# One-bank accumulators and a fixed order of copies, casts and sums in the first chunk of an up projection

## The chip, the cores and the metric

The kernel runs on one core of a Trainium2 chip. The metric is the time of one execution in microseconds (us): the median of three runs before the change is 1266.63 us (1265.53 to 1266.91). One execution was also taken by the hardware profiler: it lasted 1267.56 us, of which its span, from the first to the last instruction, is 1265.8 us.

## The reference

One decoder layer in float32 over 1024 tokens and 16 prepended meta tokens, width 1024. What matters here is its last third, the ConvFFN:

```python
up = causal_dwconv(h @ ffn_w_up, ffn_dw, ffn_dw_b)      # 1024 -> 2 * 2816, then 3 taps
u, g = jnp.split(up, 2, axis=-1)
f = (jax.nn.gelu(g, approximate=False) * u) @ ffn_w_down
return layer_norm(DEEPNORM_ALPHA * h + f, ln2_g, ln2_b)
```

`h` is the output of the first layer norm, which follows the product with `w_out`. All the rest (attention, convolution branch, gates) comes before and is not touched.

## The kernel before

Every large product is made of two rounded halves of each operand: `hi` is a cast to a narrower float format, `lo` is the rest, and three matmuls (hi by hi, hi by lo, lo by hi) stand for one in float32. ScalarE makes each `hi` by a copy (CAST in the profile), VectorE each `lo` by a subtraction.

**The up projection** (loop at L1512) goes over 22 chunks of 128 columns of `u` with the 128 columns of `g` that belong to them. A chunk is computed by Strassen's scheme (in Winograd's form): seven products, of blocks of `h` (or sums of blocks) by blocks of the weights (or sums of them), in the fixed order B11, B21, T2, T4, T1, T3, B22. Here they are called products 1 to 7, and their weights W1 to W7. Each has 12 matmuls per half of the tokens: 4 blocks of 128 rows, three matmuls each, in the order (W hi, h hi), (W hi, h lo), (W lo, h hi). The halves of the tokens are `sub` 0 (258 columns) and `sub` 1 (256 columns).

**Accumulators.** A chunk has four: V4 (tile `pw`), X (`px`), Z (`pz`) and Y (`py`), each 1024 floats wide, that is two PSUM banks, with sub 0 in the first bank and sub 1 in the second (L1513, `at` at L1520). X takes products 1, 3 and 6 on top of one another. ScalarE copies it out after each (`copy`, L1544, its instruction at L1546): to `u13`, to `u2`, and to `u13` again. Y takes products 5 and 7, with a copy to `c22` in between. VectorE adds up the four results `c11`, `c22`, `c21`, `c12` (`tt`, L1540, instruction L1542).

**Chunk 0 is special.** It is computed in two passes, first sub 1, then sub 0 (`passes`, L1514), since the last block of rows of `h` (row block 5, which belongs to sub 0) comes out of the product with `w_out` only just before. Between products 3 and 4 of the first pass, TensorE transposes that block (`turn`, called at L1557; transposes at L1323), into the banks of V4 and Z that hold sub 0 (that is, into V4 and Z as tiles). ScalarE scales the result out of them (L1336). Then the seven operands of sub 0 are formed and split: differences on VectorE (`bsub`, L1235), `hi` on ScalarE (L1226) and `lo` on VectorE (L1231), both in `bsplit` (L1222). They go to the buffers RHC, RHO, OA and RX.

**Weights.** `up_weights` (L1369) is a generator over all chunks. Of a chunk's four blocks it splits the first two as they are (W1, W2) and the fourth (W4). It forms three sums (L1383 to L1385, VectorE, instruction L1373), splits the last of these as W3, then W5, forms a fourth sum (L1389), and splits W6 and W7. `wsplit` (L1347) does a split: cast at L1355, `lo` at L1356, into a ring of ten places in RHO and `w`. Raw weights come by two DMAs of 512 KB per chunk into `wr`, which has two buffers. In front of the loop the seven weights of chunk 0 are asked for (L1510). In the loop each product of the last pass first asks until nine are ready (`w_ahead(9)`, L1525). So in the second pass of chunk 0, product 1 asks for W1 and W2 of chunk 1, and product 2 for the next one formed, W4.

**After a chunk** come, for each of its four results, a convolution of three taps (`conv_ffn`, L1459: one ScalarE instruction L1461, two VectorE instructions L1462 and L1463), for two of them a gelu (ScalarE, L1467), and two products (VectorE, L1471) that are stored by DMA to `fd`. The DMAs that load weights and store results all stand in the queue of SyncE. VectorE also forms sums of the down projection's operands (L1494 to L1497, from chunk 2 on).

**What sets the order.** A scheduler places the instructions of each engine by their rank (`rank`, L139: lower goes first, otherwise program order), as their inputs come ready by its own reckoning. `after(a, b)` (L133) fixes that `a` stands behind `b` on its engine, without a wait. `line` (L1207) chains the VectorE work on the operands of sub 0 and of the weights of chunk 0 in the order of the program, and `high` (L1227) chains four of the seven casts on ScalarE: those of T2, T4, T1 and T3.

Of the kernel before, what the change touches and what calls it, by code (L numbers as in the profile page):

```python
# [23 lines left out]
F = mybir.dt.float32  # L24
R = mybir.dt.float32r
AF = mybir.ActivationFunctionType
OP = mybir.AluOpType
AX = mybir.AxisListType

P = 128  # L30
# [30 lines left out]
SUB = [(0, 258), (258, HW)]  # L61
# [51 lines left out]
def tile_hybrid_layer(  # L113
# [3 lines left out]
    nc = tc.nc  # L117
    PSUM = bass.MemoryType.PSUM

    def dram(ap, offset, dims):  # L120
        return bass.AP(tensor=ap.tensor, offset=ap.offset + offset, ap=[list(d) for d in dims])

    def load(o, i):
        return nc.sync.dma_start(out=o, in_=i)
# [8 lines left out]
    def after(ins, first):  # L133

        tc.add_manual_dep(ins.ins, first.ins.name, mybir.DependencyInfo(
            mybir.DependencyClass.NoSync, mybir.DependencyReason.SCHED_ONLY), reason="order of work")
# [603 lines left out]
    ins = load(vd, dram(v1d, 0, [[0, P], [J_LEN, NH], [1, J_LEN]]))  # L740
# [17 lines left out]
    for g in range(NKV):  # L758
# [3 lines left out]
        for lo in (0, 64):  # L762
            for o, i in ((Kx[g][lo:, :, 16:144], kr[lo:, 16:T].rearrange("p (n c) -> p n c", c=P)),
                         (Kx[g][lo:, :, 0:16], kr[lo:, 0:16].unsqueeze(1).to_broadcast([P - lo, NB, 16]))):
                if lo == 0:
                    ins = nc.vector.tensor_copy(o, i)
                else:
                    ins = nc.vector.tensor_tensor(o, i, f32(o), OP.subtract)
# [8 lines left out]
    src = ps[:64, :P].rearrange("p (g d) -> p g d", d=HD)  # L777
    nc.scalar.copy(vm[:64, :, 0], src)
    nc.vector.tensor_tensor(vm[:64, :, 1], src, f32(vm[:64, :, 0]), OP.subtract)
    for q4 in range(2):  # L780
        ps = pat.tile([P, 512], F, name="ps_v4", tag="t", bufs=2)
        for i in range(4):
            c = NMETA + (q4 * 4 + i) * P
            after(nc.tensor.transpose(ps[:, i * P:(i + 1) * P], vT[:, c:c + P], ident), q1[-1])
        src = ps[:, :].rearrange("p (n g d) -> p n g d", g=2, d=HD)
        for g in range(NKV):
            hi, lo = (V[:, q4 * 4:q4 * 4 + 4, g, i] for i in range(2))
# [22 lines left out]
    for h in range(NH):  # L810
        g, r = divmod(h, 4)
        o = ps[:2, h * 16:(h + 1) * 16]
        ins = nc.tensor.matmul(o, q0[g][0][:, r, 0:2], Kx[g][:, 0, 0:16], start=True, stop=False)
# [138 lines left out]
    for g, (a, b) in enumerate(UG):  # L952
        with rank(RK_EVAC):
            means[g] = pat.tile([P, 512], F, name="ps_m", tag="st"[g % 2], bufs=2)
            ins = nc.tensor.matmul(means[g][:, :b - a], ones, csum[:, a:b], start=True, stop=True)
# [32 lines left out]
    sums, rstd, roots, silus = {}, {}, [], []  # L988
# [139 lines left out]
    for m in range(KC):  # L1128
        hi, lo = weights([P, KC, P], lambda raw: load(raw, w_ab[m]))
# [65 lines left out]
    B11, B21, BT2, BT1, BT3, BT4, B22 = range(7)  # L1195
# [9 lines left out]
    lined, high = [], []  # L1205
# [16 lines left out]
    def bsplit(sub, q, src, cs=slice(None)):  # L1222
        with rank(RK_SUMS):
            hi, lo = (bsum(sub, q, hl)[:, :, cs] for hl in range(2))
            src = wide(src)[:, :, cs]
            ins = nc.scalar.copy(hi, src)  # L1226
            if (sub, q) in ((0, BT2), (0, BT4), (0, BT1), (0, BT3)):  # L1227
                if high:
                    after(ins, high[-1])
                high.append(ins)  # L1230
            line(nc.vector.tensor_tensor(lo, src, f32(hi), OP.subtract))  # L1231
# [86 lines left out]
    def turn(i, r, n, ins, banks=None, behind=None, upper=False):  # L1318
        with rank(RK_TURN):
            for j, k0 in enumerate((4, 0) if upper else (0, 4)):  # L1320
                ps = banks[j] if banks else pat.tile([P, 512], F, name="ps_h", tag="s", bufs=2)
                for k in range(4):
                    ins = nc.tensor.transpose(ps[:, k * P:(k + 1) * P], r[:, (k0 + k) * P:(k0 + k + 1) * P], ident)  # L1323
                    if behind:
                        after(ins, behind[-1])
                        behind.append(ins)
                for k in range(k0, k0 + 4):
                    src = ps[:, (k - k0) * P:(k - k0) * P + n]
                    if n < P:
                        dst = edge[:, 0, k]  # L1330
                    else:
                        h, jj = divmod(i, 4)
                        sub = 0 if jj < 2 else 1
                        a = 2 + jj * P - SUB[sub][0]
                        dst = h1F(sub, h, k)[:, a:a + P]
                    nc.scalar.activation(dst, src, AF.Identity, bias=b1col(k), scale=g1col(k))  # L1336
                    if i == 3:
                        nc.scalar.activation(edge[:, 1, k], src[:, P - 2:P], AF.Identity, bias=b1col(k), scale=g1col(k))
        return behind[-1] if behind else None
# [7 lines left out]
    def wsplit(src):  # L1347
        i = ring_next[0]
        ring_next[0] += 1
        i %= len(RING)  # L1350
        if RING[i] is None:
            RING[i:i + 2] = wsp_flat()
        t = RING[i]
        hi, lo = t[:, 0:512], t[:, 512:1024]
        nc.scalar.copy(hi, src)  # L1355
        ins = nc.vector.tensor_tensor(lo, src, f32(hi), OP.subtract)  # L1356
        if pinned_w[0]:
            line(ins)
        elif ring_next[0] <= 10:
            after(ins, formed[0])  # L1360
        return hi, lo
# [31 lines left out]
                rows = w_rows(c + 1)  # L1393
            yield p3

    pinned_w, formed = [True], []
    w_stream = up_weights()
    w_ready = []

# [42 lines left out]
    last_rows = rows  # L1442
# [2 lines left out]
    ps_stack.close()  # L1445
    wo_stack.close()
    up_stack = ExitStack()
    pup = up_stack.enter_context(tc.tile_pool(name="pup", bufs=1, space=PSUM, reuse_waits="tile"))
    ft_next = [0]

    def ftmp():
# [4 lines left out]
    c11, c21, u2 = (FA[:, 4128 + i * HW:4128 + (i + 1) * HW] for i in range(3))  # L1456
    c12, c22, u13 = (RT[:, i * HW:(i + 1) * HW] for i in range(3))
# [51 lines left out]
    last_mm, copied = [], []  # L1509
    w_first(7)  # L1510
    pinned_w[0] = False
    for c in range(FC):  # L1512
        V4, X, Z, Y = (pup.tile([P, 1024], F, name=n, tag=n) for n in ("pw", "px", "pz", "py"))  # L1513
        passes = ((1,), (0,)) if c == 0 else ((0, 1),)  # L1514
        for subs in passes:
            last = subs == passes[-1]
            w_next = iter(range(7))
            a, b = SUB[subs[0]][0], SUB[subs[-1]][1]

            def at(t):  # L1520
                return t[:, 254 + a:254 + b]

            def prod(q, bank, first):
                if last:
                    w_ahead(9)  # L1525
                    ah, al = w_ready.pop(0)
                else:
                    ah, al = w_ready[next(w_next)]
                for sub in subs:
                    o = bank[:, 254 + SUB[sub][0]:254 + SUB[sub][1]]  # L1530
                    for k in range(4):
                        ks = slice(k * P, (k + 1) * P)
                        for j, (x, hl) in enumerate(((ah, 0), (ah, 1), (al, 0))):
                            ins = nc.tensor.matmul(o, x[:, ks], bmat(sub, q, hl, k), start=first and k + j == 0,  # L1534
                                                   stop=k == 3 and j == 2, skip_group_check=not first)
                            if k + j == 0 and last_mm:
                                after(ins, last_mm[-1])
                    last_mm.append(ins)

            def tt(*x):  # L1540
                with rank(RK_CHAIN):
                    return nc.vector.tensor_tensor(*x)  # L1542

            def copy(*x):  # L1544
                with rank(RK_CHAIN):
                    copied.append(nc.scalar.copy(*x))  # L1546

            prod(B11, X, True)
            copy(u13[:, a:b], at(X))
            prod(B21, Z, True)  # L1550
            if last and c not in (0, FH + 1):
                sums_load(c - 1 if c <= FH else c - 2)
            tt(c11[:, a:b], at(Z), u13[:, a:b], OP.add)
            prod(BT2, X, False)
            copy(u2[:, a:b], at(X))
            if not last:
                turn(5, *last_rows, (V4, Z), last_mm, True)  # L1557
                for q in (B11, B21):
                    split_of(0, q, LATE)
                form_t2(0, LATE)  # L1560
                formed.append(lined[-1])
                form_t4(0, LATE)
                form_t3(0, LATE)
                for q in (BT2, BT4, BT1, BT3, B22):
                    split_of(0, q)
            if last:
                g0 = gelu(conv_ffn(c11, FC + c))
            prod(BT4, V4, True)
            prod(BT1, Y, True)
            copy(c22[:, a:b], at(Y))  # L1570
            prod(BT3, X, False)
            copy(u13[:, a:b], at(X))
            ins = tt(c22[:, a:b], c22[:, a:b], u13[:, a:b], OP.add)
            if last and c not in (0, FH + 1):
                sums_form(c - 1 if c <= FH else c - 2, ins)
            tt(c21[:, a:b], u13[:, a:b], at(V4), OP.subtract)
            prod(B22, Y, False)
            tt(c12[:, a:b], at(Y), u2[:, a:b], OP.add)
            if last:
                f1 = conv_ffn(c22, c)  # L1580
                f_out(c, 0, g0, conv_ffn(c21, c))
                f_out(c, 1, gelu(conv_ffn(c12, FC + c)), f1)
# [9 lines left out]
    X, Z = ([D8[j] for j in b] for b in ((0, 1, 6, 7), (4, 5, 2, 3)))  # L1592
# [240 lines left out]
```

## Time and profile before

| what | value |
|---|---|
| median of 3 runs | 1266.63 us |
| the profiled execution | 1267.56 us, span 1265.8 us |
| VectorE, ScalarE busy | 1073.6 us (85%), 592.5 us (47%) |
| granted TensorE clock, mean | 0.997 |
| stretch 600 to 700 us: TensorE, VectorE, ScalarE busy | 98.50, 92.02, 58.05 us |
| stretch 700 to 800 us: TensorE, VectorE, ScalarE busy | 100.00, 93.42, 51.62 us |

In rows of the timeline, the first two numbers are start and duration in us; "x12" is twelve instructions in a row, whose duration is then that of all of them; in brackets stands the idle time of the engine before, and what ended it. Consecutive instructions of one engine overlap a little, so what one of them takes of the engine's time is the distance from its start to the next one's start. Lines are those of the kernel before. In the kernel after, the loop's lines stand 1 to 8 further down.

### The profile page before, as it was taken

What the parts mean: (1) busy time and instruction counts of PE and PEld (TensorE: products, weight loads), DVE (VectorE), ACT (ScalarE), POOL (GpSimd) and SP (SyncE); (2) the same over time, 40 slices, a digit from 0 to 9 for tenths busy, and PEclk for the clock granted to TensorE, in tenths of its full rate; (3) what the DMA queues carried; (4) which work ended last, traced back from release to release, by engine and by line L of the source; (5) the groups of instructions that cost most, each with busy time, mean ns of one, the idle gap of its engine ahead of it and who ended that gap; (6) DMA issues with size and microseconds to landing.
All of it is one profiled execution on the core that took longest, in us unless ns stands there. A gap on an engine that the chain in (4) does not pass through costs nothing.

```text
span 1265.8 us, 23035 instructions
## 1 busy us (share of the span) xinstructions
PE 1251.5 (99%) x9186; PEld 1183.6 (94%) x9186; DVE 1073.6 (85%) x1854; ACT 592.5 (47%) x1095; POOL 8.1 (1%) x9
## 2 busy tenths in 40 slices
PE   8999999999999999999999999999999999999997
PEld 7999999999999999788899999999999998888886
DVE  7888999999978476548899999998889887896697
ACT  7532355655473223335665555554455544445330
POOL 0000000001000000000000000000000000000000
PEclk9999999999999999999999999999999999999999
DMA  6375643332438364222145555453454567998712
GB/s 254 103 256 144 178 111 97 105 92 80 124 90 218 111 181 126 84 84 84 67 139 198 198 184 210 165 209 126 159 205 169 192 218 254 389 360 326 267 66 83
DMA packets 98701, 212.19 MB, mean 168 GB/s; under 512 B 11411, under 2 KB 38611, under 8 KB 98338
## 3 DMA queue, kind: packets, MB, share of 16 engines
q1 hardware_dynamic: 84474, 199.64, 47.3%
q10 hardware_dynamic: 14120, 11.08, 2.8%
q8 instruction: 72, 1.18, 0.4%
q14 instruction: 35, 0.29, 0.1%
HBM read 150.29 MB, written 62.70 MB: 168 GB/s over the span
## 4 chain that ended last, share of the span: by engine, by line
PE 87%; DVE 7%; DMA 3%; ACT 2%; issue 1%; SPq 0%; DVEq 0%; ACTq 0%
PE px L1534 12%; PE ps_x L1679 9%; PE ps_z L338 8%; PE ps_z L342 8%; PE py L1534 8%; PE ps_z L341 8%; PE ps_z L1679 5%; PE pz L1534 4%; PE pw L1534 4%; PE ps_p L342 2%; PE ps_p L338 2%; PE ps_p L341 2%; PE ps_w L342 2%; PE ps_w L338 2%; PE ps_w L341 2%; PE ps_z L556 2%
## 5 line engine op out<-in xcount | busy, mean ns | idle before, releaser
L342 PE MATMUL ps_z<-RHC,w 128*128 128x256 f32 (+2 forms) x864 | 244.6, 283 | 0.0
L338 PE MATMUL ps_z<-RHO,w 128*128 128x256 f32 (+2 forms) x864 | 244.3, 283 | 0.2 <-ACT FA L734 0.2
L341 PE MATMUL ps_z<-RHO,w 128*128 128x256 f32 (+2 forms) x864 | 243.1, 281 | 0.0
L338 PEld LDWEIGHTS ps_z<-RHO,w 128*128 128x128 f32 x864 | 162.5, 188 | 2.0 <-ACT FA L705 0.7
L341 PEld LDWEIGHTS ps_z<-RHO,w 128*128 128x128 f32 x864 | 162.6, 188 | 0.7
L342 PEld LDWEIGHTS ps_z<-RHC,w 128*128 128x128 f32 x864 | 162.6, 188 | 0.4
L725 DVE SCALAR_TENSOR_TENSOR FA<-cin,cdw,FA 128x1026 f32<-128x1026 f32 x120 | 152.3, 1279 | 0.7
L1356 DVE TENSOR_TENSOR RHO<-wr,RHO 128x512 fp32r<-128x512 f32 x94 | 63.6, 684 | 7.7 <-ACT RHO L1355 7.5
L1355 ACT CAST RHO<-wr 128x512 fp32r<-128x512 f32 x94 | 56.8, 620 | 25.6 <-DVE wr L1373 12.0
L300 ACT CAST w<-wr 128x1024 fp32r<-128x1024 f32 x37 | 38.7, 1047 | 61.0 <-PE ps_z L342 45.0
L734 ACT ACTIVATE FA<-ps_z,colr 128x258 f32<-128x258 f32 (+1 forms) x64 | 30.2, 473 | 69.5 <-PE ps_z L342 55.3
L1373 DVE TENSOR_TENSOR wr<-wr 128x512 f32<-128x512 f32 x88 | 59.9, 681 | 0.1
L303 DVE TENSOR_TENSOR w<-wr,w 128x1024 fp32r<-128x1024 f32 x37 | 45.1, 1218 | 16.2 <-ACT w L300 14.3
L1546 ACT COPY FA<-px 128x514 f32<-128x514 f32 (+2 forms) x23 | 13.2, 572 | 74.0 <-PE px L1534 74.0
L1356 DVE TENSOR_TENSOR w<-wr,w 128x512 fp32r<-128x512 f32 x60 | 40.5, 684 | 4.9 <-ACT w L1355 4.7
L1534 PE MATMUL px<-OA,RHO 128*128 128x258 f32 x324 | 43.2, 282 | 0.0
L1461 ACT ACTIVATE FA<-OB,coll 128x512 f32<-128x512 f32 x44 | 35.9, 815 | 14.9 <-DVE OB L1542 14.8
L1355 ACT CAST w<-wr 128x512 fp32r<-128x512 f32 x60 | 36.3, 618 | 13.2 <-DVE wr L1373 6.4
L1534 PE MATMUL px<-RHC,RHO 128*128 128x258 f32 (+1 forms) x312 | 41.1, 281 | 0.5 <-ACT OB L1546 0.5
L1534 PE MATMUL px<-OC,RHO 128*128 128x256 f32 x324 | 41.5, 277 | 0.0
L1546 ACT COPY OB<-px 128x514 f32<-128x514 f32 (+2 forms) x46 | 26.2, 569 | 32.2 <-PE px L1534 31.8
L1534 PEld LDWEIGHTS px<-OA,RHO 128*128 128x128 f32 x324 | 40.5, 189 | 0.2 <-ACT OB L1546 0.2
(442 smaller groups left out, 3295.5 us busy)
## 6 DMA issues: line engine op xcount, KB each, us to landing
wr<-in_w_up_dram SPq DMA_DIRECT2D x44, 512.0 KB, 3.6
wr<-in_w_z_dram SPq DMA_DIRECT2D x29, 512.0 KB, 3.7
OB<-in_w_down_dram SPq DMA_DIRECT2D x24, 512.0 KB, 4.9
fd<-FA SPq DMA_DIRECT2D x44, 256.0 KB, 2.1
FA<-sd SPq DMA_DIRECT2D x15, 512.0 KB, 8.7
qt<-qd SPq DMA_DIRECT2D x28, 256.0 KB, 4.1
OB<-td SPq DMA_DIRECT2D x14, 512.0 KB, 9.8
sgd<-FA ACTq DMA_DIRECT2D x48, 128.0 KB, 2.7
```

The costliest lines, as they stand in the source:

```text
L300: ins = nc.scalar.copy(hi, raw)
L303: return nc.vector.tensor_tensor(lo, raw, f32(hi), OP.subtract)
L338: ins = nc.tensor.matmul(ps, al, bh, start=i == 0, stop=False)
L341: nc.tensor.matmul(ps, ah, bh, start=False, stop=False)
L342: last = nc.tensor.matmul(ps, ah, bl, start=False, stop=i == n - 1)
L725: nc.vector.scalar_tensor_tensor(acc[c], cin[:, j:j + U], wc, acc[c], OP.mult, OP.add)
L1355: nc.scalar.copy(hi, src)
L1356: ins = nc.vector.tensor_tensor(lo, src, f32(hi), OP.subtract)
L1373: ins = nc.vector.tensor_tensor(*x)
L1534: ins = nc.tensor.matmul(o, x[:, ks], bmat(sub, q, hl, k), start=first and k + j == 0, stop=k == 3 and j == 2, skip_group_check=not first)
L1546: copied.append(nc.scalar.copy(*x))
L1679: nc.tensor.matmul(banks[i], l[:, ts], r[:, ws], start=first and a and x + k == 0, stop=z and x == len(ops) - 1 and k == 2, skip_group_che ...
```

## The change

In chunk 0 each of the four accumulators becomes a pair of tiles of one bank each, one per sub, in a pool of its own that is closed at chunk 1, where the old tiles of two banks return. The transposes of row block 5 go to the tiles of sub 0. ScalarE gets a fixed order around it: the cast of B22 joins the chain behind that of T3; in the second pass the copy of X after product 1 stands behind the cast of T4 and ahead of the cast of T1; the casts of chunk 1's W1, W2 and W4 stand behind the cast of T3. On VectorE, three sums of the first pass (`c22`, `c21`, `c12`) stand behind the `lo` of T1.

```diff
-            if (sub, q) in ((0, BT2), (0, BT4), (0, BT1), (0, BT3)):
+            if (sub, q) in ((0, BT2), (0, BT4), (0, BT1), (0, BT3), (0, B22)):
                 if high:
                     after(ins, high[-1])
                 high.append(ins)
...
-        nc.scalar.copy(hi, src)
+        w_high.append(nc.scalar.copy(hi, src))
...
-    pinned_w, formed = [True], []
+    pinned_w, formed, w_high = [True], [], []
...
-    pup = up_stack.enter_context(tc.tile_pool(name="pup", bufs=1, space=PSUM, reuse_waits="tile"))
+    halves_stack = ExitStack()
+    pup = halves_stack.enter_context(tc.tile_pool(name="puh", bufs=1, space=PSUM, reuse_waits="tile"))
...
     for c in range(FC):
-        V4, X, Z, Y = (pup.tile([P, 1024], F, name=n, tag=n) for n in ("pw", "px", "pz", "py"))
+        if c == 1:
+            halves_stack.close()
+            pup = up_stack.enter_context(tc.tile_pool(name="pup", bufs=1, space=PSUM, reuse_waits="tile"))
+        V4, X, Z, Y = ([pup.tile([P, 512], F, name=f"{n}{i}", tag=f"{n}{i}") for i in range(2)] if c == 0 else
+                       pup.tile([P, 1024], F, name=n, tag=n) for n in ("pw", "px", "pz", "py"))
...
-            def at(t):
-                return t[:, 254 + a:254 + b]
+            def at(t, sub=None):
+                x, y = (a, b) if sub is None else SUB[sub]
+                if c == 0:
+                    return t[subs[0]][:, 0:256] if subs[0] else t[0][:, 254:512]
+                return t[:, 254 + x:254 + y]
...
             prod(B21, Z, True)
+            if last and c == 0:
+                after(copied[-1], high[1])
+                after(high[2], copied[-1])
+                for ins in w_high[7:]:
+                    after(ins, high[3])
...
-                turn(5, *last_rows, (V4, Z), last_mm, True)
+                turn(5, *last_rows, (V4[0], Z[0]), last_mm, True)
...
             copy(c22[:, a:b], at(Y))
+            if not last:
+                for ins in w_high[7:]:
+                    after(ins, copied[-1])
...
-            tt(c21[:, a:b], u13[:, a:b], at(V4), OP.subtract)
+            sums = [ins, tt(c21[:, a:b], u13[:, a:b], at(V4), OP.subtract)]
             prod(B22, Y, False)
-            tt(c12[:, a:b], at(Y), u2[:, a:b], OP.add)
+            sums.append(tt(c12[:, a:b], at(Y), u2[:, a:b], OP.add))
+            if not last:
+                for ins in sums:
+                    after(ins, lined[-3])
```

The number of instructions of each kind on each engine, and the order on TensorE, are the same before and after.

2 lines of the change are left out of this document (1 added, 1 removed).

## The prediction

> **What bounds the kernel now.** I read the page first (busy times, the chain that ended last), then who TensorE waited for, then the timelines of TensorE and VectorE from 603 to 654 us.
>
> ```profile
> PE 1251.5 (99%) x9186; PEld 1183.6 (94%) x9186; DVE 1073.6 (85%) x1854; ACT 592.5 (47%) x1095; POOL 8.1 (1%) x9
> PE 87%; DVE 7%; DMA 3%; ACT 2%; issue 1%; SPq 0%; DVEq 0%; ACTq 0%
> ```
>
> TensorE is busy nearly all the time and carries the chain. Whatever keeps it idle is paid in full, and nothing else costs. In the stage that the change touches it has two waits:
>
> ```profile
> PE pw L1534 <- ACT FA L1336: 1.0, 1, 1.0
> PE px L1534 <- ACT OB L1546: 0.5, 1, 0.5
> ```
>
> ```profile
> 603.89 1.04 PE L1323 MATMUL ps_h<-coll,OB 128*128 128x128 f32 x8
> 604.68 0.48 PE L338 MATMUL ps_w<-OA,RHO 128*128 128x512 f32 x1
> ...
> 614.49 0.60 PE L1323 MATMUL pw<-coll,OB 128*128 128x128 f32 x4
> 615.04 0.66 PE L1323 MATMUL pz<-coll,OB 128*128 128x128 f32 x4
> 616.68 1.68 PE L1534 MATMUL pw<-RHC,RHO 128*128 128x256 f32 x12 [0.98 <-ACT FA L1336]
> 618.20 1.58 PE L1534 MATMUL py<-OC,w 128*128 128x256 f32 x12
> ...
> 621.02 1.57 PE L1534 MATMUL py<-RHC,w 128*128 128x256 f32 x12
> 623.11 1.70 PE L1534 MATMUL px<-RHC,RHO 128*128 128x258 f32 x12 [0.51 <-ACT OB L1546]
> ...
> 629.21 1.61 PE L1534 MATMUL py<-OA,w 128*128 128x258 f32 x12
> ...
> 633.55 1.60 PE L1534 MATMUL px<-RHC,w 128*128 128x258 f32 x12
> ...
> 639.22 1.60 PE L1534 MATMUL px<-OA,RHO 128*128 128x258 f32 x12
> ```
>
> The reader is to see the path of chunk 0: transposes at 614.49, four more products of sub 1, seven of sub 0 from 623.11, chunk 1 from 633.55, and product 3 of chunk 1 at 639.22. That last row decides below.
>
> **What the change takes away.** The first wait: product 4 may not write V4 while ScalarE still reads the transposes out of it, though they lie in the other bank. The second: X may not be started for sub 0 before ScalarE has copied sub 1 out. With one tile per bank neither remains; in the new order of instructions these two matmuls have no such wait. Without stalls the stretch from 614.49 to 633.55 would be: eight transposes in 0.79 (603.89 to 604.68), four products of sub 1 at 1.41 (618.20 to 621.02 is two), seven of sub 0 at 1.45 (629.21 to 633.55 is three), 0.79 + 5.64 + 10.15 = 16.6 against 19.1. So **up to 2.4 us** are to be had: the two waits, and the slow restarts behind them. I take all of it; the lower end is nothing. Product 3 of chunk 1 is then asked for at 639.22 - 2.4 = 636.8.
>
> For that, the operands of sub 0 must come earlier, and two kinds of ScalarE's casts matter:
>
> ```profile
> 620.65 1.11 ACT L1226 CAST OA<-OB 128x1032 fp32r<-128x1032 f32 x1
> 632.62 1.14 ACT L1355 CAST RHO<-wr 128x512 fp32r<-128x512 f32 x2
> ```
>
> In the new order they do: three `lo` of weights (L1356) leave VectorE's row ahead of them. The narrowest place is ScalarE's copy of X after product 3. Three casts of weights (0.62 long, 0.52 from start to start) now stand between the cast of B22 and it, and by my count it ends about 0.4 before TensorE wants X for product 6. That is covered, but barely.
>
> **What the change moves.** Pinning the operands and sums of chunk 0 first pushes the weights of chunk 1 back, and the scheduler puts chunk 0's convolutions ahead of them. VectorE's new row, with the kernel before's line numbers, from the `lo` of T2 to the `lo` of W3 of chunk 1:
>
> ```
> L1231 T2, L1231 T4, L1542, L1231 T1, L1542 x3, L1231 T3, L1231 B22,
> L1356 W1, L1356 W2, L1356 W4, L1462, L1542 x3, L1373, L1463, L1462, L1373,
> L1462, L1462, L1463, L1356, L1373, L1463, L1356, L1463,
> L1542 (514 wide), L1373, L1471, L1356 W3
> ```
>
> Before, the same stretch was this (W3 is the row at 636.32):
>
> ```profile
> 619.70 0.69 DVE L1235 TENSOR_TENSOR OB<-FA 128x512 f32<-128x512 f32 x1
> ...
> 622.72 1.23 DVE L1231 TENSOR_TENSOR OA<-OB,OA 128x1032 fp32r<-128x1032 f32 x1
> 623.86 0.69 DVE L1356 TENSOR_TENSOR RHO<-wr,RHO 128x512 fp32r<-128x512 f32 x1
> 624.47 0.42 DVE L1542 TENSOR_TENSOR OB<-py,FA 128x256 f32<-128x256 f32 x1
> 624.80 0.42 DVE L1542 TENSOR_TENSOR OB<-OB 128x256 f32<-128x256 f32 x1
> ...
> 636.32 0.68 DVE L1356 TENSOR_TENSOR RHO<-wr,RHO 128x512 fp32r<-128x512 f32 x1
> 636.92 0.74 DVE L1462 SCALAR_TENSOR_TENSOR FA<-OB,coll,FA 128x512 f32<-128x512 f32 x1
> 637.58 0.75 DVE L1462 SCALAR_TENSOR_TENSOR FA<-FA,coll 128x512 f32<-128x512 f32 x1
> ```
>
> W3's `lo` ended at 637.0, 2.2 before TensorE asked at 639.22. From start to start, one `lo` of an operand takes 1.14 (622.72 to 623.86), one instruction of 512 columns 0.60, a sum of 258 columns 0.33, a convolution step 0.66 (636.92 to 637.58).
>
> VectorE in the new row starts at about 621.6. T2's operand is formed at 619.70 to 620.39 as before; ScalarE's cast of it goes off at once and lasts 1.11. The two `L1235` that follow end at about 621.7 too. From there on I find no wait longer than 0.1 in the row (the sum `c11` waits for product 2 of sub 0 at about 624.0), so the work adds up: 5 x 1.14 + 7 x 0.33 + 8 x 0.66 + 12 x 0.60 = 5.70 + 2.31 + 5.28 + 7.20 = 20.5. With 0.1 for the wait and 0.1 for the full length of the last one, W3's `lo` is ready at **642.3**, 5.3 later than before, and wanted about 2.4 sooner. By the two orders of instructions, what now stands ahead of it is mostly six more convolution steps (eight against two: 4.0), two of the weights' `lo`, the 514-wide sum of chunk 1 and one L1471 (0.6 each).
>
> TensorE has the first two matmuls of product 3 once W3's `hi` is cast. That cast waits for the third L1373, which ends seven instructions (4.3) before W3's `lo`, at 638.0, and takes 0.62: about 638.7. The third matmul needs the `lo`. It would have run at 636.8 + 0.24 = 637.0 and runs at 642.3, so **5.3 are lost**, and 0.1 at the restart (1.68 against 1.58 above). By this alone: -2.4 + 5.4 = **+3.0 us**.
>
> **The clock.** TensorE then stands almost still for 5.5 us: 1.9 idle, two matmuls, 3.4 idle. The trace shows what follows such a stretch, at its start:
>
> ```profile
> 8.00:11.42 3.42, 1.00 (x7) 0.84 (x8) 2.71 (x12) 2.58 (x5) 0.00 (x0) 1.00 1.01 411
> 11.42:14.83 3.41, 3.38 (x13) 2.58 (x12) 2.12 (x6) 2.35 (x6) 0.00 (x0) 0.50 1.03 418
> 14.83:18.24 3.41, 3.41 (x21) 2.83 (x20) 2.84 (x6) 2.62 (x5) 0.00 (x0) 1.00 1.01 405
> 615.58:618.99 3.41, 2.43 (x21) 2.31 (x20) 2.43 (x6) 3.41 (x10) 0.00 (x0) 1.00 0.69 227
> ```
>
> ```profile
> 12.73 1.27 PE L553 MATMUL ps_z<-FA,wr 128*128 128x272 f32 x2
> 15.42 0.62 PE L553 MATMUL ps_z<-FA,wr 128*128 128x272 f32 x2
> ```
>
> (Columns: window, length, TensorE busy, its weight loads, VectorE, ScalarE, GpSimd, granted clock, DMA share, GB/s.) A window of 3.4 us with 1.00 busy was followed by one at clock 0.50, in which the same two matmuls took 1.27 instead of 0.62; a busy window brought 1.00 back. With 2.43 busy the clock stayed. A stretch of 5.5 us with under half a microsecond of work fills most of one such window wherever the windows lie. So I expect half the clock behind it, until a window has been busy. A window needs somewhere between 1.00 and 2.43 of work to count as busy. At the least, then, 1.0 us runs at half speed, at the most 2.43 that did not count and a whole window of 3.41 behind it, 5.8; the middle is 3.4. Half of that is lost: **0.5 to 2.9, and I take 1.7**. No loss at all is the lower end of the cost.
>
> [...]
>
> **Covered elsewhere.** The first load of chunk 2's weights now stands in SyncE's queue behind a store of chunk 0's result, which VectorE releases at about 642: so it goes off at about 642.6. A second store, two loads of `w_down` and the second weight load follow. By the page these land in:
>
> ```profile
> wr<-in_w_up_dram SPq DMA_DIRECT2D x44, 512.0 KB, 3.6
> OB<-in_w_down_dram SPq DMA_DIRECT2D x24, 512.0 KB, 4.9
> ```
>
> The loads land by about 646 and 650. Chunk 2 comes seven products of 2.83 (633.55 to 639.22 is two) behind 633.55, so at 653.4, with the shift at 656, and its W3 is wanted at 662; three sums and four splits in between are 4.2 us of VectorE. Without that slack a load would be paid, up to 3.6. From chunk 7 on, the order of the weights and convolutions is the old one. The loop over `w_high[7:]` in the first pass is empty, since seven weights have been split by then.
>
> **The rivals.**
> 1. *The stall without the clock loss*: +3.0, so 1269.6. For it: the row shows short matmuls at the start, not this stage. Chance 0.19.
> 2. *VectorE is in time*, the only rival that ends faster: the stall vanishes and the two waits' gain stays, -2.4, 1264.2. It decides at one point, W3's `lo` before 636.9; for that 5.3 us of the 20.5 would have to be absent or overlapped. For it: before, 2.2 us were in hand. Against: every row of that stretch shows VectorE busy from start to start. Chance 0.04.
> 3. *A shorter stall*: 32 instructions, each 0.05 faster than in the rows of this one execution, are 1.6 less, the gap is 3.9, and no window is empty enough for the clock. +1.4, 1268.0. Chance 0.06.
> 4. *A second stall* in chunk 2, where a weight load comes too late: up to 3.6 more, in the middle 1.8, 1273.1. Chance 0.07.
> 5. *The tiles do not free TensorE* (another wait takes the place): no gain of 2.4, yet W3 still comes at 642.3, with a shorter stall of 3.1. As W3 sets the end, the time is the forecast's, with the clock loss somewhat less likely. It adds no case of its own.
>
> **How the numbers follow.** Forecast: 1266.63 + 3.0 + 1.7 = **1271.3** (the profiled execution: 1267.56 + 4.7 = 1272.3, span 1270.5). Chance 0.64; its own range by the clock is 1270.1 to 1272.5. About 0.2%, 2.5 us, is what a measurement of this kernel can tell from no change, so slower means over 1269.2. Faster: rival 2, 0.04. Within: rival 3 and a quarter of rival 1 (whose 1269.6 lies close to that bound), 0.11. Slower: the rest, 0.85. The range takes in the forecast, rival 1 and half of rival 4: 1269.0 to 1273.1.
>
> **What would show it.** In the profile after: no wait on L1336 at product 4 and none on X at product 1 of sub 0; chunk 1 starts at about 631.1; a wait on VectorE's `lo` (the line of `wsplit`) of about 3.4 and one on ScalarE's cast of about 1.9, both at product 3 of chunk 1; VectorE without a gap from 622 to 642; a window of granted clock 0.5 behind. The prediction is wrong if W3's `lo` comes before 637, if the clock stays at 1.00, or if chunk 2 waits.

## The result, and the profile after

The kernel after takes 1273.78 us (median of 6 runs, 1272.35 to 1274.39), the kernel before, run beside it, 1266.75 (6 runs, 1265.53 to 1267.14). The ratio is 1.0057, with a 95% interval of 1.0045 to 1.0069: 7.0 us slower, and 0.7 above the end of the predicted range. The profiled execution took 1273.22 us, its span is 1271.4, its mean granted clock 0.994 (before: 0.997).

Where did the time go? First, whom TensorE waited for in the kernel after (columns: total us, times, longest):

```profile
PE px L1542 <- DVE RHO L1356: 2.9, 1, 2.9
...
PE px L1542 <- ACT RHO L1355: 2.0, 1, 2.0
...
PE py L1542 <- ACT OB L1554: 1.0, 1, 1.0
PE px L1542 <- ACT OB L1554: 0.4, 1, 0.4
```

The two waits of before (1.0 on L1336, 0.5 on the copy of X) are gone. Four new ones stand in their place: two on W3 (its cast and its `lo`), which were forecast, and two on copies of accumulators (L1554), which were not. TensorE's timeline of the kernel after shows where they are:

```profile
614.50 0.60 PE L1323 MATMUL pw<-coll,OB 128*128 128x128 f32 x4
...
631.15 1.60 PE L1542 MATMUL px<-RHC,w 128*128 128x258 f32 x12
...
638.96 0.80 PE L1542 MATMUL px<-OA,RHO 128*128 128x258 f32 x2 [1.97 <-ACT RHO L1355]
642.64 2.52 PE L1542 MATMUL px<-OA,RHO 128*128 128x258 f32 x10 [2.88 <-DVE RHO L1356]
644.95 1.92 PE L1542 MATMUL px<-OC,RHO 128*128 128x256 f32 x12
...
649.52 1.61 PE L1542 MATMUL py<-OA,RHO 128*128 128x258 f32 x12
...
656.33 1.70 PE L1542 MATMUL py<-RX,RHO 128*128 128x258 f32 x12 [1.01 <-ACT OB L1554]
...
665.45 1.69 PE L1542 MATMUL px<-OA,w 128*128 128x258 f32 x12 [0.37 <-ACT OB L1554]
666.98 1.54 PE L1542 MATMUL px<-OC,w 128*128 128x256 f32 x12
```

Chunk 1 starts at 631.15, that is 16.65 after the transposes; before it was 633.55 - 614.49 = 19.06. So 2.4 us are won there. Product 3 of chunk 1 then stands still (638.96 and 642.64), as the W3 rows of ScalarE and VectorE say:

```profile
638.28 0.62 ACT L1355 CAST RHO<-wr 128x512 fp32r<-128x512 f32 x1 [0.71 <-DVE wr L1373]
```

```profile
641.89 0.69 DVE L1356 TENSOR_TENSOR RHO<-wr,RHO 128x512 fp32r<-128x512 f32 x1
```

The `hi` is ready at 638.9, the `lo` at 642.58 (forecast: 638.7 and 642.3). What follows ran slowly: ten matmuls in 2.52. The kernel after in windows of 3.41 us, laid on the two points at which its granted clock changes here, 638.93 and 645.76 (columns as in the prediction: length, busy us of TensorE, its weight loads, VectorE, ScalarE, GpSimd, granted clock, DMA share, GB/s):

```profile
635.52:638.93 3.41, 1.46 (x13) 1.26 (x12) 3.41 (x7) 2.66 (x5) 0.00 (x0) 1.00 0.00 0
638.93:642.35 3.42, 0.80 (x2) 0.50 (x2) 3.42 (x6) 1.93 (x3) 0.00 (x0) 0.50 0.00 0
642.35:645.76 3.41, 3.12 (x14) 3.12 (x15) 2.76 (x5) 0.61 (x1) 0.00 (x0) 0.50 0.82 223
645.76:649.17 3.41, 3.41 (x31) 3.41 (x30) 0.84 (x2) 1.50 (x4) 0.00 (x0) 1.00 1.00 288
```

The window with 1.46 of 3.41 busy was followed by one at half clock (0.50), the one with 0.80 too, and only the third, with 3.12 busy, by the full clock (1.00). From 642.64 to 645.76 TensorE worked at a granted clock of 0.50: ten matmuls took 2.52, where before twelve of the same took 1.60 (639.22). That too was forecast.

The two last waits were not. SyncE's queue and ScalarE in the kernel after:

```profile
642.61 0.33 SPq L124 DMA_DIRECT2D wr<-in_w_up_dram  x1
643.22 0.33 SPq L124 DMA_DIRECT2D fd<-FA  x1
643.58 2.93 SPq L124 DMA_DIRECT2D OB<-in_w_down_dram  x2
646.63 15.06 SPq L124 DMA_DIRECT2D wr<-in_w_up_dram  x3
```

```profile
647.68 1.14 ACT L1355 CAST w<-wr 128x512 fp32r<-128x512 f32 x2 [1.91 <-DMA wr<-in_w_up_dram]
648.73 0.58 ACT L1554 COPY FA<-px 128x514 f32<-128x514 f32 x1
653.07 0.62 ACT L1355 CAST w<-wr 128x512 fp32r<-128x512 f32 x1 [3.76 <-DMA wr<-in_w_up_dram]
655.17 0.62 ACT L1355 CAST RHO<-wr 128x512 fp32r<-128x512 f32 x1 [1.48 <-DVE wr L1373]
655.70 0.58 ACT L1554 COPY OB<-py 128x514 f32<-128x514 f32 x1
```

The two weight loads of chunk 2 go off at 642.61 and 646.63, with a store and two loads of `w_down` between them, and are waited for until 647.7 and 653.07. The last row is the copy of Y after product 5 of chunk 1. Its product had ended at 652.5 (its second half starts at 650.98 and lasts 1.53), but it stands on ScalarE behind two casts of chunk 2's weights, one waiting for the second load, the other for a sum of VectorE. Product 7 waits for the copy (656.33), and the copy of X for chunk 2 is late in turn (665.45).

### The profile page after: what moved, and what is told of

Same layout as the page of the kernel before. It is cut to its first block, busy times and chain, and to the rows that moved or that the text cites. A ratio compares the mean times of both kernels' runs of the same rounds, so it can differ in the third digit from the quotient of the medians.

```text
span 1271.4 us, 23047 instructions
## 1 busy us (share of the span) xinstructions
PE 1252.5 (99%) x9186; PEld 1185.4 (93%) x9186; DVE 1073.9 (84%) x1854; ACT 591.2 (46%) x1095; POOL 8.1 (1%) x9
## 4 chain that ended last, share of the span: by engine, by line
PE 93%; DVE 3%; ACT 2%; DMA 1%; issue 1%; SPq 0%; DVEq 0%; ACTq 0%
PE px L1542 14%; PE py L1542 9%; PE ps_x L1698 9%; PE ps_z L338 8%; PE ps_z L342 8%; PE ps_z L341 7%; PE ps_z L1698 7%; PE pw L1542 5%; PE pz L1542 4%; PE ps_p L342 2%; PE ps_p L338 2%; PE ps_p L341 2%; PE ps_w L338 2%; PE ps_w L342 2%; PE ps_w L341 2%; PE ps_z L556 2%
## 5 line engine op out<-in xcount | busy, mean ns | idle before, releaser
L1554 ACT COPY FA<-px 128x514 f32<-128x514 f32 (+2 forms) x23 | 13.1, 571 | 79.3 <-PE px L1542 79.3
L1355 ACT CAST w<-wr 128x512 fp32r<-128x512 f32 x60 | 36.3, 617 | 18.1 <-DMA wr<-in_w_up_dram 10.2
L1554 ACT COPY OB<-px 128x514 f32<-128x514 f32 (+2 forms) x46 | 26.1, 566 | 32.5 <-PE px L1542 32.4
```

The lines of the kernel that those rows point to most:

```text
L1355: w_high.append(nc.scalar.copy(hi, src))
```

## The experiments

All times below are medians; the kernel before, run beside them, took 1266.36, 1266.46 and 1266.37 in the three sets of runs. One measure serves for all traces: how long after the transposes of row block 5 (the row of L1323 at 614.50 above) TensorE starts product 5 of chunk 1, and the second half of product 3 of chunk 2. In the kernel after these are 649.52 - 614.50 = 35.02 and 666.98 - 614.50 = 52.48. Before they are 30.36 and 45.86, and what lies between them, 15.50, is the same work without a wait.

### Which part of the change does it

**Tiles alone.** The kernel after without the four orders.

```diff
-            if (sub, q) in ((0, BT2), (0, BT4), (0, BT1), (0, BT3), (0, B22)):
+            if (sub, q) in ((0, BT2), (0, BT4), (0, BT1), (0, BT3)):
...
-            if last and c == 0:
-                after(copied[-1], high[1])
-                after(high[2], copied[-1])
-                for ins in w_high[7:]:
-                    after(ins, high[3])
...
-            if not last:
-                for ins in sums:
-                    after(ins, lined[-3])
```

> The kernel after with the four edits of order taken back: only the one-bank tiles of chunk 0 are left. Theory (the fixed order makes the loss, by pushing W3 of chunk 1 behind chunk 0's convolutions): W3's low part comes early enough again, no wait on VectorE at product 3 of chunk 1, no window at half clock in the up projection, and the time is the kernel before's within 1.5 us, 1265.3 to 1268.3; what the tiles free at product 4 is partly lost again at product 7 of the first pass, where ScalarE's copy of Y now stands behind casts of weights. Rival (the tiles themselves, or their pool's change at chunk 1, make the loss): W3 is late here too, and the time stays above 1271.

1266.79 us (1265.34 to 1267.04), ratio 1.0001 [0.9992, 1.0010]: no difference. The two old waits are gone, and two others, each behind a copy of ScalarE, have come at product 7 of sub 1 and product 3 of sub 0 (1.1 and 0.7). The tiles by themselves neither win nor lose.

**Orders alone.** The kernel before with these same lines added.

> The kernel before with the edits of order alone, its accumulators still two banks wide. Theory: W3's low part of chunk 1 is late by about 4 us at product 3, with a window at half clock behind, and the two waits of the kernel before at product 4 stay: slower than before by 4 to 7 us, 1270.8 to 1273.8. Rival (the tiles make the loss): as the kernel before, 1266 to 1267.5.

1273.29 us (1272.45 to 1274.95), ratio 1.0060 [1.0047, 1.0072]. TensorE's waits in this kernel:

```profile
PE px L1534 <- DVE RHO L1356: 3.2, 1, 3.2
...
PE pw L1534 <- ACT FA L1336: 1.0, 1, 1.0
PE pw L1534 <- DVE FA L1542: 1.0, 1, 1.0
```

The wait on W3's `lo` is there without the tiles, so the orders make the first stall: product 5 of chunk 1 comes 35.57 after the transposes. The second stall is not there (product 3 of chunk 2, second half, at 51.07, which is 15.50 later); a copy of X costs 0.9 in chunk 3 instead.

**W3 ahead of the convolutions.** The kernel after, with the first VectorE step of each of chunk 0's four convolutions behind W3's `lo` (the eleventh weight that is split; `w_low` collects the `lo` in `wsplit`).

```diff
...
+        w_low.append(ins)
...
-        nc.vector.scalar_tensor_tensor(t, cc[:, 1:HW - 1], ffw(1, o), t, OP.mult, OP.add)
+        ins = nc.vector.scalar_tensor_tensor(t, cc[:, 1:HW - 1], ffw(1, o), t, OP.mult, OP.add)
+        if o in (0, FC):
+            after(ins, w_low[10])
```

> The kernel after, with one more fixed order: the eight convolution steps of chunk 0 on VectorE stand behind the low part of chunk 1's W3. Theory (W3's place in VectorE's row is the cause, and the clock and the later waits follow from it): product 3 of chunk 1 no longer waits, the clock stays at 1.00, the gain of 2.4 us at chunk 0 stays: 1264.4 (1263.7 to 1265.5). Rival (the stall comes back elsewhere, since VectorE's work is the same and only turned around: the sums of chunk 0 or chunk 2's weights are late then): 1266 to 1270, with a new wait of TensorE in chunk 1 or 2.

1264.84 us (1262.88 to 1265.82), ratio 0.9987 [0.9979, 0.9996]: 1.5 below before and 9 below the kernel after. It is the fastest version here. In this kernel TensorE has no wait in the up projection, and its product 3 of chunk 1 and the W3 row read:

```profile
637.45 1.60 PE L1545 MATMUL px<-OA,RHO 128*128 128x258 f32 x12
```

```profile
636.45 0.69 DVE L1356 TENSOR_TENSOR RHO<-wr,RHO 128x512 fp32r<-128x512 f32 x1
```

The `lo` ends at 637.14, 0.3 ahead of the product. So the whole loss hangs on W3 standing behind convolution steps on VectorE, as the prediction had it. What remains is the gain: product 5 of chunk 1 comes 27.95 after the transposes, the forecast 2.4 ahead of before, and the second half of product 3 of chunk 2 comes 43.80 after them, 2.06 ahead. The median is only 1.5 lower.

**Without the held casts.** The kernel after without one order.

```diff
-                for ins in w_high[7:]:
-                    after(ins, high[3])
```

> The changed kernel without one of its four orders: the casts of weights from the eighth on are no longer held behind the cast of T3. Theory (this order is the one that pushes the weights of chunk 1, W3 among them, behind the convolutions): no wait on W3's lo; but casts now stand ahead of the copies that the orders pin, so TensorE waits on copies or operands in chunk 0 or 1 instead, some 1.5 to 3.5 in all: 1266.0 to 1268.5. Rival A (the pinned sums and the earlier B22 push W3 back): the W3 waits stay, 1272 to 1274. Rival B (each order alone is harmless and all are needed for the loss): 1264.4, faster than before.

1271.17 us (1268.81 to 1271.67), ratio 1.0032 [1.0020, 1.0045], above the expected range. The mechanism is the expected one: no wait on W3 at all. The price is not. Product 7 of chunk 1 in this kernel waits for the copy of Y. The copy, its product and the windows around it are these:

```profile
650.50 0.62 ACT L1355 CAST RHO<-wr 128x512 fp32r<-128x512 f32 x1 [0.64 <-DVE wr L1373]
651.02 0.58 ACT L1554 COPY OB<-py 128x514 f32<-128x514 f32 x1
```

```profile
651.66 2.40 PE L1542 MATMUL py<-RX,RHO 128*128 128x258 f32 x12 [2.34 <-ACT OB L1554]
653.85 2.45 PE L1542 MATMUL py<-RHC,RHO 128*128 128x256 f32 x12
656.14 1.62 PE L1542 MATMUL px<-RHC,w 128*128 128x258 f32 x12
```

```profile
648.95:652.37 3.42, 1.08 (x10) 0.89 (x9) 3.00 (x6) 2.21 (x4) 0.00 (x0) 1.00 0.12 40
652.37:655.78 3.41, 3.41 (x19) 3.41 (x18) 2.28 (x5) 1.28 (x3) 0.00 (x0) 0.50 0.75 276
```

The two halves of product 7 take 656.14 - 651.66 = 4.48 us where those of other products take 2.83: the granted clock was 0.50 at this place too, from 652.37 to 655.78, 1.65 us that the expectation had left out. So the copy of Y of chunk 1 can be late without any stall at W3: here both loads of chunk 2's weights had landed by 644.01, where the last cast that waits for them starts, and the copy stands behind casts that wait for VectorE's sums.

**Without the held sums.** The kernel after without the order of the three sums (`sums`, last lines of the first diff).

> The changed kernel without another of its orders: the sums of sub 1 are no longer held behind the last operand of sub 0. Theory (the held casts make the loss, the sums only add a little): W3's lo still waits, 0.1 to 0.5 shorter than 2.9; 1272.3 to 1273.8. Rival (the sums, held back, are what makes VectorE's row too long): no W3 wait, 1264.4 to 1266.5.

1270.38 us (1269.53 to 1271.35), ratio 1.0030 [1.0018, 1.0042]: below the expected range. W3's wait stays (1.6 and 2.6 in this trace), but its third matmul runs 27.14 after the transposes, against 642.64 - 614.50 = 28.14 in the kernel after, 1.0 sooner. The three sums stand ahead of W3's `lo` in both kernels, so it is not their 0.33 each. VectorE's rows up to that `lo` differ in one instruction: the sum of chunk 1 that is 514 wide (0.60) stands ahead of it in the kernel after (at 640.09, the `lo` at 641.89) and behind it here (at 641.51, the `lo` at 640.91). The other 0.4 are two short gaps of VectorE in the kernel after (ahead of the rows at 620.44 and 624.21), which the free sums fill. The second stall is gone as well: the copy of Y stands ahead of one more cast, and the cast ahead of it starts at 650.76, not at 653.07. So the held casts put W3 behind the convolutions, and the held sums add 1.0 to the first stall.

### What the half clock costs

**Dummies in the stall.** The kernel after, with 46 matmuls of 254 columns ahead of product 3 of chunk 1, into columns of V4 that nobody reads.

```diff
...
+            if c == 1:
+                for n in range(46):
+                    ins = nc.tensor.matmul(V4[:, 0:254], warm_w[:, 0:P], bmat(0, B11, 0, 0)[:, 0:254],
+                                           start=True, stop=True, skip_group_check=True)
+                    after(ins, last_mm[-1])
+                    last_mm.append(ins)
             prod(BT2, X, False)
```

> The kernel after, with 46 further matmuls of 254 columns between products 2 and 3 of chunk 1, written to columns of V4 that nothing reads: they fill 5.4 us, the time in which TensorE would stand still, so that it is busy and the wait for W3 is the same. Theory (half clock costs about 1.5 us behind the stall): no window below 1.00 in the up projection, product 3 starts at the same 642.6, and the time falls by 1.2 to 2.2 us, to 1271.6 to 1272.6. Rival (the granted clock in the rows costs nothing, all the loss is waiting): the time stays at 1273.3 to 1274.3.

1270.29 us (1268.90 to 1270.95), ratio 1.0032 [1.0019, 1.0044], 3.5 below the kernel after, not 1.2 to 2.2. In this trace:

```profile
635.85 5.68 PE L1573 MATMUL pw<-RHC,RHO 128*128 128x254 f32 x46
641.37 1.74 PE L1546 MATMUL px<-OA,RHO 128*128 128x258 f32 x12
```

The dummies fill the stall, product 3 behind them has twelve matmuls in 1.74, the granted clock is 1.00 from 645 to 653 (in the two later kernels with dummies from 628.7 to 656), and product 5 comes 33.62 after the transposes, against 35.02: the half clock took 1.4. The rest of the 3.5 is in the main the second stall, which is absent here: no copy is waited for in chunks 1 and 2. How the loads go with dummies is seen in the last kernel that has them, where the copy of Y is held ahead of the cast as well: its second weight load of chunk 2 goes off at 644.23, 30.3 after the transposes at 613.90 (32.1 in the kernel after), since the two issues of `w_down` ahead of it take 1.1 us and not 2.9. Why these issues are shorter with the dummies no run shows. Product 3 itself comes no sooner for the dummies: the stall is VectorE's.

### The second stall

**The loads in another order.** The kernel after, with the first two loads of `w_down` issued behind the second weight load of chunk 2.

```diff
...
             after(load(t[h], (w_dn_v if i < FH else fd)[j + h * FH]),
-                  loads[-1] if loads else f_stores[-1])
+                  w_loads[5] if i == 0 else loads[-1] if loads else f_stores[-1])
```

> The changed kernel, with one more order: the first two loads of w_down (for the down projection) are issued behind the second weight load of chunk 2 instead of ahead of it. Nothing else moves. Theory (the changed kernel pays a second stall because that weight load, behind 1 MB of w_down, lands at 653.05 and ScalarE's copy of Y stands behind its cast): the two waits at products 7 and 3 (1.0 and 0.4) go, with their restarts 2.0 us; the first stall (2.0 and 2.9 at W3) and the half clock stay. 1273.8 - 2.0 = 1271.8, between 1271.2 and 1272.4. Rival (the load is late because its issue waits for a store of chunk 0, or because the transfers are slow in that stretch whatever their order): both waits stay, 1273.2 to 1274.2.

1271.99 us (1270.67 to 1273.01), ratio 1.0042 [1.0029, 1.0056]. The time is in the expected range, but the trace does not bear the theory out: product 7 still waits 0.9. In this kernel ScalarE shows why:

```profile
650.10 0.62 ACT L1355 CAST w<-wr 128x512 fp32r<-128x512 f32 x1 [0.98 <-DMA wr<-in_w_up_dram]
...
652.21 0.62 ACT L1355 CAST RHO<-wr 128x512 fp32r<-128x512 f32 x1 [1.00 <-DVE wr L1375]
652.99 0.62 ACT L1355 CAST RHO<-wr 128x512 fp32r<-128x512 f32 x1 [0.16 <-DVE wr L1375]
654.20 0.62 ACT L1355 CAST w<-wr 128x512 fp32r<-128x512 f32 x1 [0.58 <-DVE wr L1375]
654.72 0.58 ACT L1556 COPY OB<-py 128x514 f32<-128x514 f32 x1
```

The load comes 2.3 sooner (its cast starts 36.3 after the transposes, not 653.07 - 614.50 = 38.6), yet the copy of Y now stands behind three casts that each wait for a sum of VectorE; in the kernel after it was one.

**The same with the dummies.**

> The same load order, and 46 dummy matmuls (254 columns, into columns that nobody reads) ahead of product 3 of chunk 1, which keep TensorE busy while W3 is late. So it has the first stall's length, and neither the half clock nor the second stall. Theory (the kernel with the dummies alone lost its second stall by chance of the transfers' timing, and the half clock is worth about 1.5): as that kernel, 1270.3, between 1269.7 and 1270.9, and 1.2 to 1.8 below the kernel with the load order alone. Rival (the half clock costs the whole 3.5 by which the dummies alone fell): 3.5 below the kernel with the load order alone, about 1268.3.

1271.02 us (1269.96 to 1272.72), ratio 1.0037 [1.0024, 1.0049], 0.1 above the expected range, and a second stall of 0.43 is left (table below). It is 0.97 below the kernel with the load order alone, with overlapping ranges: nearer to the theory than to the rival's 3.5, and by itself not decisive.

**The first load ahead of the store.**

```diff
...
         f_stores.append(load(fd[c, :, h * 512:(h + 1) * 512], t))
+        if c == 0:
+            after(f_stores[-1], w_loads[4])
```

> The changed kernel with the first weight load of chunk 2 issued ahead of the stores of chunk 0's result, not behind the first of them; the second load then goes ahead of one of the loads of w_down. Theory (the second stall begins with that store, which VectorE releases at 642): the loads land 2 us or more sooner than 647.7 and 653.0, no wait at products 7 and 3, the first stall stays: 1271.8, between 1271.2 and 1272.4. Rival (ScalarE's order alone makes it: the copy of Y stands behind casts that wait for VectorE's sums of the weights): the wait at product 7 stays, 0.5 to 1.0, and the time is 1272.6 to 1273.8.

1271.88 us (1271.72 to 1272.63), ratio 1.0045 [1.0031, 1.0058]; the wait at product 7 is gone, the one at product 3 of chunk 2 (0.4) is not. The time is in the expected range, but again not for the expected reason: the first load does not go off sooner. It goes off at 641.71, which in this kernel is the moment in which W3's `lo` ends. SyncE's waits say so (from 625 to 660 us):

```profile
SPq L124 <- DVE RHO L1356: 23.7, 2, 23.3
```

The load waits 23.3 us for a `lo` of VectorE, the last reader of the raw buffer that it fills. The store ahead of it was never what held it. In the kernel after it is the same: W3's `lo` ends at 642.58, the load goes off at 642.61, 28.11 after the transposes in both kernels. Nor does the copy of Y come sooner:

```profile
654.81 0.58 ACT L1558 COPY OB<-py 128x514 f32<-128x514 f32 x1
```

That is 654.81 - 613.60 = 41.21 after the transposes (613.60 in this trace), against 655.70 - 614.50 = 41.20 in the kernel after. Product 7 does not wait for it only because TensorE comes 1.4 later here, behind a longer half clock. The end is the same: 52.57 and 52.48 in the table below.

**The copy ahead of the cast.** The kernel after, with one order more.

```diff
             copy(c22[:, a:b], at(Y))
+            if c == 1:
+                after(w_high[16], copied[-1])
```

> The changed kernel with ScalarE's copy of Y after product 5 of chunk 1 held ahead of the cast of chunk 2's third weight (the one that waits for the second load); the loads stay where they are, and the scheduler orders later chunks a little differently. Theory (the copy behind that cast is what TensorE waits for): no wait at product 7 however late the load is, 1271.8, between 1271.0 and 1272.6; the first stall stays, and a weight of chunk 2 may be waited for in its place, no more than 0.5. Rival (the weights of chunk 2 are themselves late): a wait on a cast or a lo of chunk 2 of 1 or more takes its place, 1273 to 1274.

1271.94 us (1271.61 to 1272.97), ratio 1.0046 [1.0034, 1.0059]. There is no wait at products 7 and 3, and none in its place. The load came no sooner (it goes off at 647.01, 32.4 after the transposes; 646.63 and 32.1 in the kernel after; from issue to landing the median of the two loads is 5.6, there 5.7). The copy did:

```profile
653.20 0.59 ACT L1554 COPY OB<-py 128x514 f32<-128x514 f32 x1 [3.51 <-PE py L1542]
653.69 0.62 ACT L1355 CAST w<-wr 128x512 fp32r<-128x512 f32 x1
```

It waits for its product alone. So ScalarE's order, with the late load and VectorE's sums ahead of the copy, is what makes the second stall. Some of the fall may be hidden: the half clock is 1.86 in this trace and 1.40 in the kernel after, so about 0.5 of the 1.96 would have been covered by that; the other 1.5 is the order.

**The same with the dummies.**

> The same, with the 46 dummy matmuls ahead of product 3 of chunk 1, so that TensorE has no half clock: the difference from the kernel with the copy held is the price of the half clock. Theory: 1.3 to 1.5 (what TensorE's positions give in the traces so far), so 1270.4, between 1269.6 and 1271.2, and no wait in chunks 1 and 2. Rival (the clock costs nothing in the end, since the next thing is late anyway): within 0.5 of the kernel with the copy held.

1270.89 us (1269.31 to 1271.30), ratio 1.0034 [1.0021, 1.0046], 1.05 below the kernel with the copy held, and no wait in chunks 1 and 2. The time is in the expected range; the difference is less than the 1.3 to 1.5 by the medians, and 1.86 by the positions in the two traces.

**The kernel after once more.**

> The changed kernel once more, without an edit, beside the next three on one chip, so that differences of 1 to 2 us between them can be read. 1273.8, between 1273.1 and 1274.5, with the second stall (products 7 of chunk 1 and 3 of chunk 2) in its trace too. Rival (the second stall hangs on how fast the loads of that one execution were): another execution is without it, and its span is 2 shorter.

1272.49 us (1271.05 to 1273.29), ratio 1.0047 [1.0035, 1.0060]: lower than expected. The second stall is in this trace too (0.7 and 0.3). Of the eleven executions of this kernel in both sets five lie below 1273.1. So differences of about 1 us between these kernels are not told by medians of five, and the positions in the traces carry more:

| kernel | product 5 of chunk 1 | half clock | product 3 of chunk 2, second half | second stall |
|---|---|---|---|---|
| before | 30.36 | none | 45.86 | none |
| after | 35.02 | 1.40 | 52.48 | 1.96 |
| after once more | 34.98 | 1.36 | 52.03 | 1.55 |
| loads in another order | 34.91 | 1.29 | 51.93 | 1.52 |
| first load ahead of the store | 36.41 | 2.79 | 52.57 | 0.66 |
| copy ahead of the cast | 35.48 | 1.86 | 50.98 | 0 |
| dummies | 33.62 | 0 | 49.12 | 0 |
| load order and dummies | 33.63 | 0 | 49.56 | 0.43 |
| copy ahead and dummies | 33.62 | 0 | 49.12 | 0 |

"Half clock" is the position of product 5 less the 33.62 that it has with dummies, "second stall" the distance between the two positions less 15.50. The two columns are not prices that add up freely: where the copy of Y is late, a longer half clock only shortens the wait for it, as the first load ahead of the store shows.

## Why the prediction was wrong, point by point

The direction and the main mechanism were right; the size was not. By the table, the kernel after is 52.48 - 45.86 = 6.62 behind at the end of the disturbed stretch.

1. **The two waits of chunk 0, -2.4.** Right: both are gone, and chunk 1 starts 2.41 sooner (19.06 - 16.65). ScalarE's copy of X, "covered, but barely", was covered: it ended at 627.76, and product 6 began at 628.26.
2. **W3's `lo` behind the convolutions, +5.4.** Right. It was forecast for 642.3 and ended at 642.58, the cast's wait was forecast at 1.9 (1.97) and that of the `lo` at 3.4 (2.88; the two matmuls ahead of it ran at half clock, 0.80 instead of the 0.50 of other traces). Steps 1 and 2 together: 33.62 - 30.36 = 3.26 in the table, against +3.0. The kernel with W3 ahead of the convolutions shows that this is the cause: with it, nothing is lost.
3. **The clock, +1.7 (0.5 to 2.9).** Right within its bounds: 1.40 in this execution, as the row of 8.00 to 11.42 foretold. Rival 1, no clock loss, is out.
4. **"Covered elsewhere".** This is the step that failed. It let the loads of chunk 2 land "by about 646 and 650" and found 12 us of slack before W3 of chunk 2. ScalarE's casts waited for them until 647.7 and 653.07: the second load was not issued until 646.63, and six transfers (two stores of 256 KB, four loads of 512 KB) are under way from 642 to 653. But the kernel with the copy held has no wait at products 7 and 3, although its loads are as late. What the step overlooked is who else stands behind such a load: on ScalarE, the copy of Y of chunk 1 stood behind the cast that waited for it, and TensorE wants that copy at once. The kernel without the held casts shows the same copy late with no stall at W3 at all. That is the second stall of rival 4 (chance 0.07), at other places: at copies in chunks 1 and 2, not at a weight of chunk 2. It is 1.96 in this execution, 1.55 in the other. Also, the load was held by its raw buffer, which W3's late `lo` frees, not by the store that the step named; the time, 642.6, was right by chance.

Forecast 4.7, plus 0.26 for steps 1 and 2, less 0.3 for the clock, plus 1.96: 6.62. By the medians it is 7.0, by the spans of the two profiled executions only 5.6 (1271.4 - 1265.8). Over the fourteen traces here the transposes start anywhere from 613.2 to 615.1, and what lies behind the last position takes 604.4 to 605.9, so times and positions can differ by 1 or more; this is not explained further. The second set of the kernel after, 1272.49, lies inside the predicted range of 1269.0 to 1273.1: that 1273.78 lies outside is in part chance, while the second stall, which the sum put at nothing, stands in both traces. Rivals 2, 3 and 5 are out: VectorE was not in time, the stall was not shorter, and the tiles did free TensorE.

One slip without effect: the section on the kernel before has product 2 of chunk 0 ask for W4 alone; by the program W3 is split there too, behind W4, so its cast is among the held ones. It waits for its sum until 638.28 in any case.

## What to carry to other kernels

A pinned order that pulls some instructions forward pushes all others back, and the scheduler may put cheap-looking work ahead of what the bound engine wants next: read each engine's new row up to the next thing that the bound engine asks for, and pin that too. When a late value also frees a buffer, follow the load that fills it, and look at what stands behind its first reader on each engine, not only at when the loaded data are wanted. Price a stall of the bound engine together with the slow stretch behind it, and as a range: behind the same waits that stretch cost 1.29 to 2.79 us here.

## What the runs showed of the hardware

The price of the half clock was not set by the stall alone. Behind the same two waits at product 3 (2.0 on the cast of W3, 3.2 on its `lo`) it was 1.29 to 2.79 us in four kernels (table). The windows of two of them show where they part. The kernel after once more:

```profile
634.11:637.52 3.41, 1.73 (x15) 1.53 (x14) 3.41 (x6) 2.69 (x5) 0.00 (x0) 1.00 0.00 0
637.52:640.94 3.42, 0.51 (x2) 0.30 (x2) 3.42 (x7) 2.11 (x4) 0.00 (x0) 1.00 0.00 0
640.94:644.35 3.41, 2.86 (x13) 2.86 (x14) 3.02 (x5) 0.40 (x2) 0.00 (x0) 0.50 0.75 201
644.35:647.76 3.41, 3.41 (x31) 3.41 (x31) 0.00 (x0) 0.76 (x2) 0.00 (x0) 1.00 1.00 378
```

The kernel with the first load ahead of the store:

```profile
637.66:641.08 3.42, 0.50 (x2) 0.30 (x2) 3.42 (x7) 2.11 (x4) 0.00 (x0) 1.00 0.00 0
641.08:644.49 3.41, 2.75 (x13) 2.75 (x14) 3.14 (x6) 0.40 (x2) 0.00 (x0) 0.50 0.41 119
644.49:647.90 3.41, 3.41 (x17) 3.41 (x17) 0.00 (x0) 0.65 (x2) 0.00 (x0) 0.50 0.93 352
```

In the second kernel the work starts 0.1 later in its window. There 2.75 busy of a window at half clock was followed by a whole further window at 0.50; in the first kernel 2.86 was followed by 1.00. At full clock, the window with 1.73 busy of 3.41 was followed by the full clock, those with 1.46 (the kernel after), 1.08 (without the held casts), 0.51 and 0.50 by half of it. The half clock lasted 3.41 us in the first kernel (640.94 to 644.35) and in the kernel without the held casts (652.37 to 655.78), twice that in the second (641.08 to 647.90) and in the kernel after (638.93 to 645.76). What sets these lengths, and where between 1.46 and 1.73, or between 2.75 and 2.86, the turn lies, no run shows.

In the burst of six transfers the weight loads take longer. The weight loads of the kernel after between 640 and 656 us (the last column is the median from issue to landing):

```profile
wr<-in_w_up_dram SPq DMA_DIRECT2D x2, 512.0 KB, 5.7
```

Over all weight loads of the kernel before it was 3.6. All transfers together moved 223 and 288 GB/s in the two windows after 642.35 of this execution, and 201 and 378 in the two after 640.94 of the other one. The casts that wait for the two loads start 33.2 and 38.6 after the transposes in this one, 33.9 and 38.2 in the other: when a load of a burst lands isn't fixed either.
